# mLSTM head normalization on GpSimd instead of ScalarE, with the heads' transposes one visit later

## The chip, the cores and the metric

The kernel runs on one core of a Trainium2 chip. The metric is the device time of one execution in microseconds; the median of three runs is compared. One execution more was recorded by the hardware profiler, and all durations below come from it. The engines are called as in the profile: PE (TensorE matmul), PEld (its weight loads), DVE (VectorE), ACT (ScalarE), POOL (GpSimd), SP (SyncE, which only issues transfers here).

## What is computed

One inference step of a two-layer streaming encoder over 1024 prompt rows and 32 sample rows, width 1024, all in float32. Layer 0 mixes by an mLSTM with 4 heads (key width 128, value width 256), layer 1 by attention over a band of chunks; each has an MLP with squared ReLU. The change lies in the mLSTM mixer, and within it in the last steps of each head:

```
num = einsum(s, v) + a * einsum(C, q)              # per chunk and head
den = s.sum + a * einsum(n, q)
h   = num / max(|den|, exp(-m_t))
mu  = h.mean(-1);  var = square(h - mu).mean(-1)   # over the 256 values of a head
h   = (h - mu) * rsqrt(var + 1e-6) * mhn_g
h   = h * sigmoid(o_pre)
y   = h @ w_out
```

The division by the denominator and the normalization over 256 values come to one scale and one shift for each row, so that the kernel applies both in one operation `hn * w + b`.

## The kernel before

The input projection of the mLSTM runs head by head. For head h, `qk_proj` makes the queries and keys (six blocks of 24 matmuls, 384, 384 and 288 columns wide, for q and for k), `v_proj` the values (nine tiles of 24 matmuls with 256 columns), and `o_proj` later the output gates, for two heads at a time. While PE does this for head h+1, the mLSTM of head h is done in between: `mlstm(h, ...)` is a Python generator, and after each block or tile of the projection `flow.tick()` advances it by one visit. The rows of a head are nine chunks: eight of 128 prompt rows and one with the 32 sample rows (chunk 8). `flow.finish(ml)` runs what is left of a generator at the end of its head.

A visit i of the loop at the end of `mlstm` does up to four things, each for another chunk:

- `scores(i)`: W = exp(...) on ACT (L666), S = k q and the transpose of k on PE (L668, L669) into one PSUM tile of the tag "tp", their product on DVE (L671), the scaled queries `qc` on POOL (L675), the weighted keys `kw` on ACT (L677).
- `values(i - 1)`: the numerators `num` (L686, L688) and the state's update `cu` (L690) on PE, into PSUM tiles of the tag "nm"; the new state on DVE (L693); mean and variance of the numerators on DVE (L705, L706); a copy of them into the SBUF tile `hn` on ACT (L708), and of the denominator (L709). With every third chunk `values` calls `scales`.
- `state_out(i - 2)`: only for the last two chunks, the transposed state `co` to memory. `co` shares the tag "hn", which has four buffers.
- `heads(c)`: two transposes of `hn` on PE (L738) into a "tp" tile, and a copy into G on ACT (L739). In visits 4, 7 and 10 it is done for two chunks, in 5, 8 and 11 for the third of the group.

`scales` works for three chunks at once on tiles of three columns: five DVE operations (L715 to L719), Ln and Exp on ACT (L720, L721), six DVE operations (L722 to L727). Then it normalizes the three `hn` in place, one operation each (L731). So the transposes of a group of three chunks hang on a chain DVE, ACT, DVE, ACT, and there are 4 heads x 3 groups = 12 such chains and 36 normalizations.

Three rings matter: "tp" has two PSUM buffers, for which S and the heads' transposes take turns; "nm" has two, for `num` and `cu`; "hn" has four SBUF buffers, so that the copy of a fifth chunk's numerators waits for the transposes of the first. For the next head, `mlstm` loads a tile `rc` by DMA and masks it on POOL (two affine_select, L645) before its first visit; W of that head reads it.

The order in which the instructions stand on an engine is not that of the code. The framework's planner lists the instructions by their dependencies, its own planned durations and the order of the code: an instruction that it does not expect to be ready is passed by later ones of the same engine that are. Once listed, an engine takes its instructions strictly in that order. In this stage the order on PE is the planner's.

The numbers of lines are those of the profile.

Of the kernel before, what the change touches and what calls it, by code (L numbers as in the profile page):

```python
# [10 lines left out]
AF = mybir.ActivationFunctionType  # L11
ALU = mybir.AluOpType
# [9 lines left out]
NT = T // P + 1  # L22
# [53 lines left out]
def trunk_kernel(ctx: ExitStack, tc: tile.TileContext, a, o):  # L76
    nc = tc.nc
# [6 lines left out]
    def raw_tile(shape, name):  # L84
        return ring.tile(shape, F32, tag="raw", name=name, bufs=3)
# [93 lines left out]
    def tpt(name):  # L179
        return pa.tile([P, 512], F32, tag="tp", name=name, bufs=2)  # L180
# [458 lines left out]
    def mlstm(h, qT, kT, vts):  # L639
# [10 lines left out]
        def geo(c):  # L650
            return (CH, c * CH, c * CH) if c < NCK else (TS, TP + 3, TP)

        def scores(c):
            L, yo, to = geo(c)
            if c == NCK:
                cl = raw_tile([P, 2, P], f"cl_{h}")
                nc.sync.dma_start(cl, a["state_C"][0, 0, h].rearrange("(j p) k -> p j k", p=P))
                ps = tpt(f"clp_{h}")
                for j in range(2):
                    nc.tensor.transpose(ps[:, j * P:(j + 1) * P], cl[:, j], ident)  # L660
                c0 = A.tile([P, 258], F32, tag="ct", name=f"ct0_{h}", bufs=3)
                nc.vector.tensor_copy(c0[:, :256], ps[:, :256])
                nc.gpsimd.tensor_copy(c0[:, 256:257], n0c[:, h:h + 1])
                live["c0"] = c0
            W = A.tile([P, P], F32, tag="W", name=f"W_{h}_{c}", bufs=3)
            nc.scalar.activation(W[:L, :L], rc[:L, 0, to:to + L], AF.Exp, bias=ae[:L, c, h:h + 1])  # L666
            pst = tpt(f"S_{h}_{c}")
            nc.tensor.matmul(pst[:L, :L], kT[:, yo:yo + L], qT[:, yo:yo + L], start=True, stop=True)  # L668
            nc.tensor.transpose(pst[:L, 256:256 + P], kT[:, yo:yo + L], ident)  # L669
            sT = A.tile([P, P], F32, tag="sT", name=f"sT_{h}_{c}", bufs=2)  # L670
            nc.vector.tensor_mul(sT[:L, :L], pst[:L, :L], W[:L, :L])  # L671
            qc = None
            if c > 0:
                qc = A.tile([P, P], F32, tag="qc", name=f"qc_{h}_{c}", bufs=2)
                nc.gpsimd.tensor_mul(qc[:, :L], qT[:, yo:yo + L], rc[:, 1, to:to + L])  # L675
            kw = A.tile([P, P], F32, tag="kw", name=f"kw_{h}_{c}", bufs=2)
            nc.scalar.activation(kw[:L], pst[:L, 256:256 + P], AF.Copy, scale=W[:L, L - 1:L])  # L677
            live[c] = (sT, qc, kw)

        def values(c):  # L680
            L, yo, to = geo(c)
            sT, qc, kw = live[c]
            vt = vts[c]
            prev = live["c0"] if c == NCK else ct.get(c - 1)
            num = nmt(f"num_{h}_{c}")
            nc.tensor.matmul(num[:L, :257], sT[:L, :L], vt[:L, :257], start=True, stop=qc is None)  # L686
            if qc is not None:
                nc.tensor.matmul(num[:L, :257], qc[:, :L], prev[:, :257], start=False, stop=True)  # L688
            cu = nmt(f"cu_{h}_{c}")
            nc.tensor.matmul(cu[:, :257], kw[:L, :], vt[:L, :257], start=True, stop=True)  # L690
            cn = ct[c] = A.tile([P, 258], F32, tag="ct", name=f"ct_{h}_{c}", bufs=3)
            if prev is not None:
                nc.vector.scalar_tensor_tensor(cn[:, :257], prev[:, :257], albc[:, h, c:c + 1], cu[:, :257],  # L693
                                               op0=ALU.mult, op1=ALU.add)
            else:
                nc.vector.tensor_copy(cn[:, :257], cu[:, :257])

            slot = c % 3
            if slot == 0:
                live["sm"] = A.tile([P, 3, 8], F32, tag="sm", name=f"sm_{h}_{c}", bufs=2)  # L700
                if c + 3 > NCK:
                    nc.gpsimd.memset(live["sm"], 1.0)
            sm = live["sm"]
            st = A.tile([P, 6], F32, tag="st", name=f"st_{h}_{c}", bufs=3)
            nc.vector.bn_stats(st[:L], num[:L, :256])  # L705
            nc.vector.bn_aggr(sm[:L, slot, 0:2], st[:L])  # L706
            hn = live[c] = A.tile([P, 256], F32, tag="hn", name=f"hn_{h}_{c}", bufs=4)
            nc.scalar.copy(hn[:L], num[:L, :256])  # L708
            nc.scalar.copy(sm[:L, slot, 2:3], num[:L, 256:257])  # L709
            if slot == 2:  # L710
                scales(c - 2, sm)

        def scales(c0, sm):
            mean, var, d, rd, v, y0, w, b = (sm[:, :, i] for i in range(8))
            nc.vector.scalar_tensor_tensor(rd, d, -1.0, ae[:, c0:c0 + 3, 32 + h], op0=ALU.mult, op1=ALU.max)  # L715
            nc.vector.tensor_max(rd, rd, d)
            nc.vector.reciprocal(rd, rd)
            nc.vector.tensor_mul(v, var, rd)
            nc.vector.tensor_mul(v, v, rd)  # L719
            nc.scalar.activation(y0, v, AF.Ln, bias=eps_hn)  # L720
            nc.scalar.activation(y0, y0, AF.Exp, scale=-0.5)  # L721
            nc.vector.tensor_mul(w, y0, y0)  # L722
            nc.vector.scalar_tensor_tensor(w, v, HN_EPS, w, op0=ALU.add, op1=ALU.mult)
            nc.vector.tensor_scalar(w, w, -0.5, 1.5, op0=ALU.mult, op1=ALU.add)
            nc.vector.tensor_mul(w, w, y0)
            nc.vector.tensor_mul(w, w, rd)
            nc.vector.scalar_tensor_tensor(b, mean, -1.0, w, op0=ALU.mult, op1=ALU.mult)  # L727
            for i in range(3):
                L = geo(c0 + i)[0]
                hn = live[c0 + i]  # L730
                nc.scalar.activation(hn[:L], hn[:L], AF.Identity, bias=sm[:L, i, 7:8], scale=sm[:L, i, 6:7])  # L731

        def heads(c):
            L, yo, to = geo(c)
            hn = live.pop(c)
            pth = tpt(f"hT_{h}_{c}")
            for j in range(2):
                nc.tensor.transpose(pth[:, j * P:j * P + L], hn[:L, j * P:(j + 1) * P], ident[:L, :L])  # L738
            nc.scalar.copy(G[:, 2 * h:2 * h + 2, to:to + L], pth[:, :256].rearrange("p (j t) -> p j t", j=2)[:, :, :L])  # L739

        def state_out(c):
            if c >= NCK - 1:
                w = 0 if c == NCK - 1 else 1
                nc.gpsimd.tensor_copy(ncol[:, 4 * w + h:4 * w + h + 1], ct[c][:, 256:257])
                ps = tpt(f"co_{h}_{c}")
                for j in range(2):
                    nc.tensor.transpose(ps[:, j * P:(j + 1) * P], ct[c][:, j * P:(j + 1) * P], ident)
                co = A.tile([P, 256], F32, tag="hn", name=f"co_{h}_{c}", bufs=4)
                nc.scalar.copy(co, ps[:, :256])
                nc.sync.dma_start(o["C_s" if w else "C_p"][0, 0, h].rearrange("(j p) k -> p j k", p=P),  # L750
                                  co.rearrange("p (j k) -> p j k", j=2))

        for i in range(NT + 3):
            if i < NT:
                scores(i)
            if 1 <= i <= NT:
                values(i - 1)
            if 2 <= i < NT + 2:
                state_out(i - 2)
            if i >= 4 and i % 3:  # L760
                for c in (i - 4, i - 3)[:3 - i % 3] if i % 3 == 1 else (i - 3,):
                    heads(c)
            yield

    def tick(*_):
# [60 lines left out]
    for h in range(1, NH):  # L826
        unit = [0]

        def after_qk():
            unit[0] += 1  # L830
            if h > 1 or unit[0] >= 3:
                flow.tick()
        if h == 1:
            ml = flow.add(mlstm(0, *qk[0], vts[0]))
        qk.append(qk_proj(h, after_qk))
        vts.append(v_proj(h, tick))
        flow.finish(ml)
        ml = flow.add(mlstm(h, *qk[h], vts[h]))
# [937 lines left out]
    bias, sbias = [], []  # L1776
# [141 lines left out]
    for gp in range(2):  # L1918
        for i in range(17):
            c = slim[gp][i // 2] if i % 2 else wide[i // 2] if i < 16 else slim[gp][8]  # L1920
            if not gp and i < 2:
                c = 7 + i
# [244 lines left out]
```

## Time and profile before

| | us |
|---|---|
| median of three runs | 2409.23 (2408.87 to 2410.61) |
| the profiled execution | 2412.41 |
| its span, first to last instruction | 2410.6 |
| granted TensorE clock, mean | 0.995 of full speed |
| stretch with the visits of `mlstm` | 110 to 386 |

Two kinds of rows are used below. A row of the waits reads "engine, tile and line that waited, what released it: us in total, times, longest". A row of the timeline reads "start, length, engine, line, operation, out <- in, shapes, how many", with the idle time before it and what ended that in brackets. PE's matmuls are pipelined: the length of one is longer than the distance to the next, so that the distance from start to start tells more.

### The profile page before, as it was taken

The numbers are of one execution on the slowest core, as the hardware profiler recorded it, in microseconds if no ns is written. First come the engines' busy times: TensorE is split into PE (matmuls) and PEld (weight loads), VectorE is DVE, ScalarE is ACT, GpSimd is POOL, SyncE is SP. The second block draws the span as 40 slices with busy tenths as digits, with TensorE's granted clock in tenths as the row PEclk, the third lists the DMA queues.
The fourth block names the chain that finished last, engine by engine and source line by source line (L and its number), as shares of the span: only waits on it lengthen the run. The fifth ranks groups of instructions, "written<-read, shape, count | busy, mean of one in ns | idle before, by whom it ended". The sixth has DMA issues, their size and how long they took to land. (4 is left out here: it accounts for less than half of the span.)

```text
span 2410.6 us, 44188 instructions
## 1 busy us (share of the span) xinstructions
PE 2342.7 (97%) x17180; PEld 2250.4 (93%) x17180; DVE 1939.0 (80%) x3903; ACT 1206.0 (50%) x2454; POOL 168.1 (7%) x320
## 2 busy tenths in 40 slices
PE   7999999999999999999999999999999999899997
PEld 4999999999999999999999987789999999899997
DVE  4888766778788789989888777756998889888778
ACT  4565557278666630101147467773776777222212
POOL 0111100000000000000000224420000000000003
PEclk9999999999999999999999999999999999999999
DMA  8343222526566896675512330051486779976642
GB/s 302 120 131 103 78 89 66 177 91 206 184 198 200 279 336 230 252 261 215 183 56 89 82 93 1 10 140 59 165 278 211 259 278 335 355 256 236 224 146 73
DMA packets 284277, 424.64 MB, mean 176 GB/s; under 512 B 15384, under 2 KB 205228, under 8 KB 278948
## 3 DMA queue, kind: packets, MB, share of 16 engines
q1 hardware_dynamic: 279860, 391.48, 48.3%
q10 hardware_dynamic: 4208, 30.35, 3.1%
q8 instruction: 135, 2.21, 0.4%
q14 instruction: 74, 0.61, 0.1%
HBM read 305.96 MB, written 118.17 MB: 176 GB/s over the span
## 5 line engine op out<-in xcount | busy, mean ns | idle before, releaser
L1082 DVE SCALAR_TENSOR_TENSOR ACX<-dn,ada,ACX 128x264 f32<-128x264 f32 (+6 forms) x664 | 281.8, 447 | 83.2 <-PE dn L1452 41.1
L1452 PE MATMUL dn<-fx,wf_d 128*128 128x264 f32 x2016 | 254.1, 285 | 6.8 <-DVE ACX L1082 3.5
L1452 PEld LDWEIGHTS dn<-fx,wf_d 128*128 128x128 f32 x2016 | 248.8, 188 | 9.0 <-DVE ACX L1082 3.0
L89 ACT CAST w_dn<-raw_dn 128x1024 fp32r<-128x1024 f32 x36 | 37.7, 1050 | 282.1 <-DVE aw L279 136.9
L118 PE MATMUL dn<-hs,w_dn 128*128 128x384 f32 (+2 forms) x512 | 161.2, 315 | 0.0
L119 PE MATMUL dn<-hs,w_dn 128*128 128x384 f32 (+2 forms) x512 | 161.0, 315 | 0.0
L120 PE MATMUL dn<-hs,w_dn 128*128 128x384 f32 (+2 forms) x512 | 156.4, 314 | 1.3 <-DVE w_dn L90 1.3
L1317 PE MATMUL up<-TF,wf_u 128*128 128x264 f32 x1056 | 143.2, 285 | 3.8 <-ACT H L1320 3.8
L1317 PE MATMUL up<-U,wf_u 128*128 128x264 f32 x1056 | 140.3, 285 | 1.7 <-ACT H L1320 1.2
L1317 PE MATMUL up<-u,wf_u 128*128 128x264 f32 x1056 | 139.7, 285 | 1.3 <-ACT wf_u L89 0.7
L279 DVE SCALAR_TENSOR_TENSOR aw<-radw,cs,aw 128x512 f32<-128x512 f32 x196 | 139.5, 743 | 1.1 <-DMA radw<-in_w_ada_dram 1.1
L1317 PEld LDWEIGHTS up<-TF,wf_u 128*128 128x128 f32 x1056 | 134.4, 189 | 4.8 <-ACT H L1320 4.6
L1317 PEld LDWEIGHTS up<-U,wf_u 128*128 128x128 f32 x1056 | 133.0, 188 | 3.0 <-ACT H L1320 1.6
L1317 PEld LDWEIGHTS up<-u,wf_u 128*128 128x128 f32 x1056 | 132.9, 188 | 1.9 <-ACT wf_u L89 0.9
L118 PE MATMUL dn<-U,w_dn 128*128 128x384 f32 (+2 forms) x416 | 129.4, 312 | 0.6 <-DVE ada L304 0.6
L119 PE MATMUL dn<-U,w_dn 128*128 128x384 f32 (+2 forms) x416 | 129.4, 312 | 0.0
L120 PE MATMUL dn<-U,w_dn 128*128 128x384 f32 (+2 forms) x416 | 125.9, 313 | 0.6 <-DVE w_dn L90 0.5
L1817 ACT ACTIVATE p<-p,mx 128x576 f32<-128x576 f32 (+9 forms) x132 | 86.6, 657 | 27.5 <-DVE mx L1814 25.2
L120 PEld LDWEIGHTS dn<-hs,w_dn 128*128 128x128 f32 x512 | 96.0, 188 | 2.0 <-DVE w_dn L90 1.8
L118 PEld LDWEIGHTS dn<-hs,w_dn 128*128 128x128 f32 x512 | 96.5, 189 | 0.1
L119 PEld LDWEIGHTS dn<-hs,w_dn 128*128 128x128 f32 x512 | 96.6, 189 | 0.0
L90 DVE TENSOR_TENSOR HL<-H,HL 128x1056 fp32r<-128x1056 f32 x64 | 80.3, 1254 | 20.0 <-ACT HL L89 19.9
(403 smaller groups left out, 7111.0 us busy)
## 6 DMA issues: line engine op xcount, KB each, us to landing
hpl<-HL SPq DMA_DIRECT2D x144, 264.0 KB
rdn_u<-in_w_up_dram SPq DMA_DIRECT2D x64, 512.0 KB
hd<-HL SPq DMA_DIRECT2D x28, 1056.0 KB
fx<-hd SPq DMA_DIRECT2D x50, 528.0 KB
radw<-in_w_ada_dram SPq DMA_DIRECT2D x24, 1024.0 KB
hd<-HM SPq DMA_DIRECT2D x28, 792.0 KB
raw_up<-in_w_up_dram SPq DMA_DIRECT2D x40, 512.0 KB
raw_dn<-in_w_down_dram SPq DMA_DIRECT2D x36, 512.0 KB
```

The lines of the kernel that those rows point to most:

```text
L89: nc.scalar.copy(dst_h, src)
L90: (eng or nc.vector).tensor_sub(dst_l, src, dst_h.bitcast(F32))
L118: nc.tensor.matmul(ps, wh, mov(0, k), start=(k == 0), stop=False)
L119: nc.tensor.matmul(ps, wh, mov(1, k), start=False, stop=False)
L120: nc.tensor.matmul(ps, wl, mov(0, k), start=False, stop=(k == nk - 1))
L279: nc.vector.scalar_tensor_tensor(acc[cnd], raw[:, k], sc, acc[cnd], op0=ALU.mult, op1=ALU.add)
L1082: nc.vector.scalar_tensor_tensor(xs, ps[:, off + o:off + o + mm_], gate[:, fc, cnd:cnd + 1], xs, op0=ALU.mult, op1=ALU.add)
L1317: nc.tensor.matmul(p, self.ws[w][:, wl, k], moving(f, tp, xl, k), start=first and k + n_ == 0, stop=k == 3 and n_ == 2, skip_group_check=n ...
L1452: nc.tensor.matmul(p, ws[w][:, wl, k], t[:, s0, xl], start=first and k + n_ == 0, stop=k == kg - 1 and n_ == 2, skip_group_check=not first)
L1817: nc.scalar.activation(z, z, AF.Exp, bias=mx[:, 0:1], scale=-1.0, accum_out=mx[:, 1:2])
```

## The change

The normalization in `scales` moves from ACT to POOL (`tensor_scalar` with two operands that hold one value for each row). `heads` moves by one visit, from 4, 5, 7, 8, 10 and 11 to 5, 6, 8, 9, 11 and 12, and within the visit from the end to the place between `scores` and `values`. The loop has one visit more.

```diff
@@ -728,7 +728,7 @@
             for i in range(3):
                 L = geo(c0 + i)[0]
                 hn = live[c0 + i]
-                nc.scalar.activation(hn[:L], hn[:L], AF.Identity, bias=sm[:L, i, 7:8], scale=sm[:L, i, 6:7])
+                nc.gpsimd.tensor_scalar(hn[:L], hn[:L], sm[:L, i, 6:7], sm[:L, i, 7:8], op0=ALU.mult, op1=ALU.add)
@@ -750,16 +750,16 @@
-        for i in range(NT + 3):
+        for i in range(NT + 4):
             if i < NT:
                 scores(i)
+            if i >= 5 and i % 3 != 1:
+                for c in (i - 5, i - 4) if i % 3 == 2 else (i - 4,):
+                    heads(c)
             if 1 <= i <= NT:
                 values(i - 1)
             if 2 <= i < NT + 2:
                 state_out(i - 2)
-            if i >= 4 and i % 3:
-                for c in (i - 4, i - 3)[:3 - i % 3] if i % 3 == 1 else (i - 3,):
-                    heads(c)
             yield
```

The 36 operations, their operands and the transposes themselves stay as they were.

## The prediction

> **What bounds the kernel now.** I read the busy shares first, then the table by stretch, then the waits.
>
> ```profile
> PE 2342.7 (97%) x17180; PEld 2250.4 (93%) x17180; DVE 1939.0 (80%) x3903; ACT 1206.0 (50%) x2454; POOL 168.1 (7%) x320
> 110.00:150.00 40.00, 39.74 (x272) 37.84 (x271) 39.59 (x89) 29.16 (x84) 5.42 (x22) 1.00 0.25 75
> 150.00:250.00 100.00, 97.36 (x671) 90.51 (x671) 82.15 (x193) 53.15 (x150) 14.55 (x41) 1.00 0.41 127
> 250.00:386.00 136.00, 134.59 (x874) 126.21 (x873) 95.77 (x246) 80.42 (x220) 13.74 (x38) 1.00 0.28 87
> 386.00:2410.00 2024.00, 1978.37 (x14791) 1920.19 (x14789) 1652.51 (x3236) 987.43 (x1891) 121.75 (x187) 1.00 0.54 184
> ```
>
> The columns of the stretches are length, then busy time of PE, PEld, DVE, ACT and POOL, granted clock, DMA share, GB/s. The mLSTM visits lie between 110 and 386 us. There PE is busy 39.74 + 97.36 + 134.59 = 271.69 of 276 us, at a granted clock of 1.00; DVE is full only in the first 40 us, ACT has 113 us free and POOL 242. After 386 us PE is busy 1978 of 2024 us. So TensorE sets the end throughout, and the change can gain only what PE waits for in the mLSTM stage. What that is:
>
> ```profile
> PEld hT L738 <- ACT hn L731: 6.5, 11, 1.5
> PE hT L738 <- ACT hn L731: 3.5, 4, 1.3
> PEld co L747 <- issue: 1.3, 4, 0.3
> PEld S L668 <- DVE y L617: 0.5, 1, 0.5
> ```
>
> The first two rows are the waits of weight load and matmul for the same event (total us, times, longest): the transposes of L738 wait for the ACT normalization of L731, in 11 of the 12 groups of three chunks, 6.5 us at most by the weight load. No other wait of PE or PEld in this stretch comes to more than 1.3 us, and the one longest wait for DVE is 0.5. **6.5 us, 0.27% of the span, is the ceiling.** L731 in its turn needs L727, the last of the small DVE operations in `scales`.
>
> How do these waits arise? Three views of one place, head 0, chunks 3 to 5 (start, length, instruction):
>
> ```profile
> 153.85 1.06 DVE L727 SCALAR_TENSOR_TENSOR sm<-sm 128x3 f32<-128x3 f32 x1
> 154.83 0.74 DVE L279 SCALAR_TENSOR_TENSOR ada_acc<-ada_room,cs,ada_acc 128x512 f32<-128x512 f32 x1
> ```
> ```profile
> 153.73 3.89 POOL L645 TENSOR_SCALAR_AFFINE_SELECT rc<-rc 128x1024 f32<-128x1024 f32 x2 [4.17 <-DMA rc<-rc_d]
> ```
> ```profile
> 154.92 0.40 ACT L666 ACTIVATE W<-rc,ae 128x128 f32<-128x128 f32 x1 [3.72 <-POOL rc L645]
> 155.23 1.57 ACT L731 ACTIVATE hn<-hn,sm 128x256 f32<-128x256 f32 x3
> ```
> ```profile
> 154.29 0.28 PE L489 MATMUL v<-w_v,U 128*128 128x256 f32 x1
> 154.40 0.28 PE L487 MATMUL v<-w_v,U 128*128 128x256 f32 x1
> 155.87 0.44 PE L738 MATMUL hT<-ident,hn 128*128 128x128 f32 x2 [1.19 <-ACT hn L731]
> ```
>
> PE runs projection matmuls 0.11 us apart until 154.40 and then has the transpose at its head, which can start at 155.87: 1.47 - 0.12 = 1.35 us are lost. L727 ended at 154.91, ACT then still had a W of the next head, the first normalization ran from 155.23 to 155.82, and PE went on 0.05 us later. So the transposes stand in PE's queue where the planner expected the normalization, and PE pays for each lateness.
>
> **Does the transpose move at all?** This decides more than the engine. In head 1 the code emits `heads(0)` in visit 4, ahead of the fifth numerators, which belong to visit 5. The trace has:
>
> ```profile
> 199.59 0.70 PE L686 MATMUL num<-vt,sT 128*128 128x257 f32 x2
> ...
> 200.56 0.60 PE L690 MATMUL cu<-vt,kw 128*128 128x257 f32 x2
> ...
> 205.10 0.28 PE L489 MATMUL v<-w_v,U 128*128 128x256 f32 x1
> 205.44 0.44 PE L738 MATMUL hT<-ident,hn 128*128 128x128 f32 x2
> ```
> ```profile
> L487 PE MATMUL v<-w_v,U 128*128 128x256 f32 x12 | 3.6, 296 | 0.0
> L489 PE MATMUL v<-w_v,U 128*128 128x256 f32 x12 | 3.4, 280 | 0.0
> L488 PE MATMUL v<-w_v,U 128*128 128x256 f32 x12 | 3.4, 280 | 0.0
> ```
>
> The fifth numerators stand ahead of the first transposes, and 36 projection matmuls (12 of each line between 200.7 and 205.3 us) lie between them; one v tile has 24. The planner has already put these transposes past the place to which the change moves them, because their input is not expected earlier. A later place in the code then binds nothing: PE has always some other matmul, and the transpose comes when the planner expects its input. Counting the numerators in the trace in this way, the new place lies behind the old one in two of the twelve groups only: the last of head 2 and the second of head 3.
>
> ```profile
> 295.56 0.28 PE L489 MATMUL v<-w_v,U 128*128 128x256 f32 x1
> 296.20 0.44 PE L738 MATMUL hT<-ident,hn 128*128 128x128 f32 x2 [0.36 <-ACT hn L731]
> ```
> ```profile
> 357.43 0.29 PE L119 MATMUL o<-U,w_o 128*128 128x288 f32 x1
> 357.87 0.44 PE L738 MATMUL hT<-ident,hn 128*128 128x128 f32 x2
> ```
>
> **The change part by part.** The rows for prices (ns: min/median/max, or mean):
>
> ```profile
> L731 ACT ACTIVATE hn<-hn,sm x36: 584/588/604, 142.6 to 377.7; 128x256 f32<-128x256 f32 x32, 32x256 f32<-32x256 f32 x4
> L1825 POOL TENSOR_SCALAR p<-p,mx 128x320 f32<-128x320 f32 x8 | 4.2, 532 | 4.3 <-DVE mx L1823 4.3
> L1825 POOL TENSOR_SCALAR p<-p,mx 128x192 f32<-128x192 f32 x8 | 3.3, 426 | 1.1 <-DVE mx L1823 1.1
> L675 POOL TENSOR_TENSOR qc<-y,rc x32: 240/458/1479, 105.0 to 354.3; 128x128 f32<-128x128 f32 x28, 128x32 f32<-128x32 f32 x4
> L675 POOL TENSOR_TENSOR qc<-y,rc 128x128 f32<-128x128 f32 x26 | 15.0, 577 | 79.4 <-PE num L688 78.8 <-DMA rc<-rc_d 0.6
> L719 DVE TENSOR_TENSOR sm<-sm x12: 121/157/420, 135.5 to 371.2; 128x3 f32<-128x3 f32 x12
> L727 DVE SCALAR_TENSOR_TENSOR sm<-sm x12: 123/166/1060, 142.4 to 376.5; 128x3 f32<-128x3 f32 x12
> ```
>
> *Place.* The two moved groups lose their waits: 0.64 - 0.12 = 0.52 and 0.44 - 0.12 = 0.32, together **-0.8 us**. What moves with a head is two transposes and one ACT copy into G, no DMA.
>
> *Engine.* 36 x 588 ns = 21 us leave ACT, which is half idle here, so that this is worth nothing in itself. On POOL one normalization should take halfway between the 426 and 532 ns of the neighbouring widths, 0.48 us (its second operation is a real addition here, which the row does not show; ends 0.43 and 0.59). Each remaining waiting group (11 - 2 = 9) gets its first chunk 0.588 - 0.48 = 0.11 us sooner: **-1.0 us**.
>
> *Queue on POOL.* The normalization waits for L727 at the head of POOL. Behind it stand `qc` (its 79 us of waiting for PE show that it is made about a visit ahead of its numerators), the two-column memsets of `vt`, the copies of `tails`, and the next head's affine_select of L645, for which that head's W on ACT waits, and the rest of ACT behind that. All but the last have a visit of slack. The other way round costs more: in the place shown above ACT runs the next head's W, which needs L645, ahead of the normalization, so the planner expects L645 first, and the normalization queues behind it. L645 ended at 157.62; plus 0.48 that is 158.10 instead of 155.82, or +2.3 us of PE wait. The order on POOL in the changed kernel is not shown, the ends are 0 and 2.3; I take half, **+1.2 us**. At the other two boundaries:
>
> ```profile
> 218.65 2.45 POOL L645 TENSOR_SCALAR_AFFINE_SELECT rc<-rc 128x1024 f32<-128x1024 f32 x2 [3.73 <-DMA rc<-rc_d]
> ...
> 287.66 1.25 POOL L645 TENSOR_SCALAR_AFFINE_SELECT rc<-rc 128x1024 f32<-128x1024 f32 x2 [3.47 <-ACT hn L731]
> ```
> ```profile
> 220.96 0.62 DVE L727 SCALAR_TENSOR_TENSOR sm<-sm 128x3 f32<-128x3 f32 x1
> ```
> ```profile
> 287.03 1.10 ACT L731 ACTIVATE hn<-hn,sm 128x256 f32<-128x256 f32 x2 [1.50 <-DVE sm L727]
> ```
>
> In head 1 L645 ended (221.10) before L727 did (221.58), in head 2 it began after the normalization: nothing there.
>
> *Port.* `qc` takes 458 ns by the median and 577 by the mean of this stretch: 0.12 us of delay beside DVE. For the nine groups of heads 0 to 2, less the one priced above, 8 x 0.12 = **+1.0 us**; ends 0 and the rival below. DVE is delayed too: L719 took 420 instead of 157 ns at worst, and 36 x 0.26 = 9.5 us of DVE time is the bound; PE hardly waits for DVE in this stretch, so I put 0 on the path, and up to 3 us in heads 0 and 1 if the DVE slack is gone.
>
> *Buffers.* `hn` has four buffers; with heads 6 to 8 held longer, the state copy `co` of visit 10 has only the buffer of the other `co` and waits for its DMA on ACT. A v tile of 24 x 0.12 = 2.8 us on PE covers that, 0 us; uncovered it is 1 us per head, by the longest of the two such waits that the kernel has now:
>
> ```profile
> ACT co L749 <- DMA out_dram<-co: 1.4, 2, 1.0
> ```
>
> *Planner.* How long it expects the POOL operation to take is not in the trace. If longer than the chip takes, every transpose comes later in PE's queue and its wait shrinks; if shorter, it grows. I take 0; ends -5 and +2 us. The stages after 386 us are replanned as well; their 46 us of PE idle may shift by a few per cent, 2 us either way.
>
> Sum: -0.8 - 1.0 + 1.2 + 1.0 = +0.4 us. The profiled execution took 2412.41 us for its span of 2410.6, so it would take 2412.8; the median of the runs is 3.18 us lower, 2409.23, and becomes **2409.6 us**. 0.2% (4.8 us) is about what a measurement of this kernel can tell from no change, so the forecast is: no change.
>
> **The rivals.**
>
> *All waits go.* If the planner allows POOL more time than it takes, or the order of the moved transposes falls better than my count, the waits vanish: about -6 us (6.5 less the 0.05 us of signal in each of 11), 2403.2 us. For it: without the 1.35 us above, the mean of the others is 0.5 us, so little is needed. Against it: the largest come from late DVE and POOL work, which stays.
>
> *GpSimd late by its queue (slower).* If at each of the three head boundaries the affine_select lands ahead of the normalization as priced for head 0, that is 3 x 2.3 + 1.0 - 1.8 = +6.1 us, 2415.3. It decides from the point at which the normalization starts over 1 us after L727 has ended. Against it: two of the three boundaries show no collision now.
>
> *GpSimd late by the port (slower).* In the place above L727 begins while L645 runs and takes 1.06 us instead of 0.17; L645 in turn took 3.89 us beside DVE. If each first normalization of heads 0 to 2 waits for one two-input DVE operation such as L279 (0.74 us), that is 9 x 0.74 = 6.7, with -1.8 and +1.2 in all +6.1 us, 2415.3 again. The Trainium skill, SBUF — State Buffer, section "Who interferes with whom", states this as a lock: GpSimd shares a port pair with VectorE, and a VectorE instruction with two SBUF inputs and a GpSimd instruction that reads SBUF exclude each other for a whole instruction, whichever starts first. The two rows agree with it; by that rule alone the change would come out slower. The median of `qc`, 458 ns in a stage in which DVE is 79% busy, says that most instructions escape, so it is a rival only.
>
> **How the numbers follow.** Forecast, within 0.2%: 0.60, its own range 2405 to 2414. All waits go: 0.22. Queue: 0.09, port: 0.09. The range takes in the centre of the first rival and most of the way to the other two: 2403 to 2414.5. Faster by over 0.2%: 0.22; within: 0.60; slower: 0.18.
>
> **What would show it.** The first transpose of head 1 still after the fifth numerators, near 205 us: the place does not bind. The wait of hT then names POOL instead of ACT, with 4 to 8 us in total. A normalization on POOL of 0.43 to 0.6 us, longer where DVE is full. Head 0's second group late behind L645, by up to 3.7 us on PE. I am wrong if the wait of hT is gone (below 1 us), if PE newly waits for ACT or DVE in this stage, or if stages after 386 us change by more than 3 us.

## The result, and the profile after

The changed kernel takes 2423.89 us (median of 6 runs, 2418.34 to 2426.57) beside 2409.05 us before (2408.44 to 2414.3): a ratio of 1.0058, interval 1.0048 to 1.0068. It is 14.8 us slower, above the predicted range (2403 to 2414.5). The profiled execution has a span of 2424.8 us.

Where the time went is read from windows that end just behind the last transposes of the mLSTM, at 379 us before and at 394 us after. The columns are those of the prediction: length, busy time of PE, PEld, DVE, ACT and POOL, granted clock, DMA share, GB/s. First the kernel before:

```profile
110.00:379.00 269.00, 264.69 (x1772) 247.70 (x1770) 214.59 (x518) 158.90 (x443) 33.71 (x101) 1.00 0.32 100
```

The changed kernel, this stretch and 2024 us behind it:

```profile
110.00:394.00 284.00, 270.45 (x1771) 251.97 (x1770) 215.05 (x518) 144.19 (x410) 60.46 (x137) 0.98 0.31 97
400.00:2424.00 2024.00, 1978.65 (x14797) 1922.37 (x14795) 1650.98 (x3237) 987.19 (x1891) 122.38 (x187) 1.00 0.54 184
```

The stretch is 15.0 us longer, and the 2024 us behind it hold what 2024 us held before (PE 1978.65 us busy, before 1978.37). All of the loss lies in the mLSTM stage. It has two parts: PE is idle 284.00 - 270.45 = 13.55 us instead of 4.31 (+9.2), and it is busy 5.8 us longer with the same number of matmuls (1771 and 1772), at a mean clock of 0.98 instead of 1.00. ACT got 14.7 us lighter, which is worth nothing here.

The waits of the changed kernel in this stage name the event that the prediction watched, now released by POOL (us, times, longest; before 6.5 and 3.5):

```profile
PEld hT L738 <- POOL hn L731: 17.7, 17, 3.2
```
```profile
PE hT L738 <- POOL hn L731: 12.5, 10, 2.7
```

One GpSimd normalization, by its line and then by stretch, heads 0 to 2 first and head 3 below:

```profile
L731 POOL TENSOR_SCALAR hn<-hn,sm x36: 544/555/1577, 141.9 to 392.2; 128x256 f32<-128x256 f32 x32, 32x256 f32<-32x256 f32 x4
```
```profile
L731 POOL TENSOR_SCALAR hn<-hn,sm 128x256 f32<-128x256 f32 x24 | 20.0, 841 | 22.2 <-DVE sm L727 22.2
```
```profile
L731 POOL TENSOR_SCALAR hn<-hn,sm 128x256 f32<-128x256 f32 x9 | 5.0, 568 | 18.1 <-DVE sm L727 18.1
```

Undisturbed it takes 0.555 us, about ACT's 0.588. In head 3 the mean is near that (0.568; one of the nine belongs to the end of head 2), in heads 0 to 2, where VectorE prepares the next head's weights and the ada products, it is 0.841.

The costliest place shows how this becomes time. The third group of head 0 in the changed kernel, as three timelines (PE, POOL, DVE):

```profile
166.95 0.28 PE L489 MATMUL v<-w_v,U 128*128 128x256 f32 x1
169.97 1.22 PE L738 MATMUL hT<-ident,hn 128*128 128x128 f32 x4 [2.75 <-POOL hn L731]
```
```profile
168.53 2.45 POOL L731 TENSOR_SCALAR hn<-hn,sm 128x256 f32<-128x256 f32 x3 [4.72 <-DVE sm L727]
```
```profile
166.45 1.22 DVE L90 TENSOR_TENSOR w_v<-raw_v,w_v 128x1024 fp32r<-128x1024 f32 x1
167.59 0.16 DVE L724 TENSOR_SCALAR sm<-sm 128x3 f32<-128x3 f32 x1
...
168.18 0.17 DVE L727 SCALAR_TENSOR_TENSOR sm<-sm 128x3 f32<-128x3 f32 x1
168.26 1.22 DVE L90 TENSOR_TENSOR w_v<-raw_v,w_v 128x1024 fp32r<-128x1024 f32 x1
```

PE had the transpose at its head from 167.2 us, when VectorE was still in L90 with four of the small operations of `scales` to come. L727 ended at 168.35. POOL started 0.18 us later, in the shadow of the next L90 (168.26 to 169.48). Its three operations took 2.45 us. The first was done just ahead of the transpose at 169.97, some 1.4 us after its start (2.45 less twice 0.55) and 0.4 us after that L90 had ended. At 0.56 us it would have been done some 0.8 us earlier.

What follows on PE, in windows of 3.41 us of the same kernel:

```profile
166.75:170.16 3.41, 0.66 (x7) 0.47 (x5) 2.64 (x6) 1.05 (x1) 1.63 (x2) 1.00 0.74 225
170.16:173.57 3.41, 3.41 (x16) 2.79 (x16) 2.02 (x4) 1.16 (x4) 0.82 (x2) 0.50 0.88 278
173.57:176.98 3.41, 3.41 (x20) 3.41 (x21) 2.17 (x4) 1.19 (x2) 0.00 (x0) 1.00 0.01 2
```

After 2.75 us of idling PE works for 3.41 us at half the clock. The stage of the changed kernel has three such spells, from 170.16, 211.12 and 231.59 us, the first and the last after the two longest gaps; the stage before has none. They hold 3.41 + 3.41 + 6.83 = 13.65 us, so they cost at most 6.8 us, and the 5.8 us of longer busy time fit that. The Trainium skill, TensorE: Matmul & The Clock Gate, Part 1, states a gate of half or full rate, set by the activity in windows of about 3.4 us; the length and the 0.50 agree with it.

### The profile page after: what moved, and what is told of

Its sections match the earlier page's. It is cut to its first block, busy times and chain, and to the rows that moved or that the text cites. A ratio compares the mean times of both kernels' runs of the same rounds, so it can differ in the third digit from the quotient of the medians.

```text
span 2424.8 us, 44232 instructions
## 1 busy us (share of the span) xinstructions
PE 2346.8 (97%) x17180; PEld 2255.8 (93%) x17180; DVE 1937.3 (80%) x3903; ACT 1189.9 (49%) x2418; POOL 192.0 (8%) x356
## 3 DMA queue, kind: packets, MB, share of 16 engines
q8 instruction: 135, 2.21, 0.4%
## 5 line engine op out<-in xcount | busy, mean ns | idle before, releaser
L90 DVE TENSOR_TENSOR HL<-H,HL 128x1056 fp32r<-128x1056 f32 x64 | 80.2, 1254 | 20.4 <-ACT HL L89 20.4
```

Source lines behind the costliest of these rows:

```text
L90: (eng or nc.vector).tensor_sub(dst_l, src, dst_h.bitcast(F32))
```

## The experiments

Theories. **A**: GpSimd's normalization comes late against the place at which the planner put the transposes: the planner expects it earlier, VectorE's two-input operations stretch it, and the gaps on PE bring half-clock spells. **B**: the moved transposes cost. **C**: GpSimd's mere presence beside VectorE costs. Ratios are to runs of the kernel before on the same chip (medians 2408.26 for e1 to e4, 2409.07 for e5, e6, e9 and e10, 2408.70 for the rest).

### Each half of the change alone: e1_engine, e2_place

e1 is the kernel before with the operation moved to POOL, e2 the changed kernel with it put back on ACT.

```diff
-                nc.scalar.activation(hn[:L], hn[:L], AF.Identity, bias=sm[:L, i, 7:8], scale=sm[:L, i, 6:7])
+                nc.gpsimd.tensor_scalar(hn[:L], hn[:L], sm[:L, i, 6:7], sm[:L, i, 7:8], op0=ALU.mult, op1=ALU.add)
```

> The kernel before with the normalization on GpSimd; the transposes stay where they were. Theory A (the added time comes from the GpSimd normalization: it ends later than the planner placed the transposes for, PE stands at hT, and the granted clock halves after such gaps): 2417 to 2426 us, wait of hT for POOL 12 us or more. Rival B (the moved transposes do it, by the order of S, num and cu and the two PSUM buffers): 2409 us within 3, wait of hT about 6.5 us as before.

> The changed kernel with the normalization back on ScalarE; the transposes stay one visit later, ahead of the numerators. A: 2406 to 2412 us, wait of hT for ACT 4 to 8 us, no half-clock spell between 110 and 386 us. B: 2417 us or more with the wait of hT well above 6.5 us.

Measured: e1 2428.18 us, ratio 1.0083 (1.0068 to 1.0098); e2 2404.71, 0.9992 (0.9983 to 1.0002). The waits and the stage of e1, then of e2:

```profile
PEld hT L738 <- POOL hn L731: 20.3, 25, 2.1
```
```profile
110.00:394.00 284.00, 269.19 (x1760) 249.95 (x1759) 213.71 (x516) 143.99 (x408) 59.94 (x137) 0.98 0.31 97
```
```profile
PEld hT L738 <- ACT hn L731: 4.9, 7, 1.2
```
```profile
110.00:377.00 267.00, 263.71 (x1771) 247.24 (x1770) 213.88 (x518) 158.15 (x445) 34.79 (x101) 1.00 0.33 103
```

The engine alone costs 19.9 us (PE idle 14.81 us, and three half-clock spells of 3.41 us), the place alone gives 3.6 back (its interval just takes in no change, and its stage has no such spell); the sum, 16.4, is near the 14.8 of the change. B falls.

Why the wait grows without a collision can be counted in e1, where the transposes have their old place in the code. Between the fifth numerators and the first transposes of head 1 stand

```profile
L487 PE MATMUL v<-w_v,U 128*128 128x256 f32 x11 | 3.3, 297 | 0.0
L489 PE MATMUL v<-w_v,U 128*128 128x256 f32 x11 | 3.1, 280 | 0.0
L488 PE MATMUL v<-w_v,U 128*128 128x256 f32 x11 | 3.1, 279 | 0.0
```

33 projection matmuls, where the kernel before had 36. The planner lists these transposes 3 x 0.117 = 0.35 us earlier, as if the normalization were faster on POOL, and on the chip it is not. The same count from fixed numerators over all twelve groups has them two or three PE instructions earlier in seven groups and 12 earlier in one, at the same place in one and 2 to 10 later in three: a tendency, not a rule.

### Another engine, a later place: e3_dve, e4_two, e6_act_two, e12_dve_place, e13_place_again

e3 is the kernel before with the operation on VectorE (first diff). e4 and e6 move the transposes two visits instead of one, with POOL and with ACT; e12 is the changed kernel with VectorE, e13 is e2 again.

```diff
-                nc.scalar.activation(hn[:L], hn[:L], AF.Identity, bias=sm[:L, i, 7:8], scale=sm[:L, i, 6:7])
+                nc.vector.tensor_scalar(hn[:L], hn[:L], sm[:L, i, 6:7], sm[:L, i, 7:8], op0=ALU.mult, op1=ALU.add)
```
```diff
-        for i in range(NT + 3):
+        for i in range(NT + 5):
...
+            if i >= 6 and i % 3 != 2:
+                for c in (i - 6, i - 5) if i % 3 == 0 else (i - 5,):
+                    heads(c)
```

> The kernel before with the normalization on VectorE, transposes as before. If it is an engine beside DVE's chain (a signal to another engine, the shared port) that is late, DVE itself, which ended the chain anyway, has neither: wait of hT 6.5 us or less, 2404 to 2410 us. If any move away from ScalarE is late because the planner counts the operation too short, the wait rises as in e1: 2415 us or more.

> The changed kernel (GpSimd) with the transposes one visit later still (visits 6, 7, 9, 10, 12, 13). If one visit did not bind because the planner expects the input later than that place, and two visits do bind: wait of hT below 5 us and 2406 to 2412 us. If the planner's expectation still decides, or the four hn buffers now hold up the numerators: wait of hT 10 us or more, 2416 us or more.

> Normalization on ScalarE as before, the transposes two visits later than before and ahead of that visit's numerators (one visit later still than in the changed kernel). Theory A: with ScalarE the place binds in five of the twelve groups and their waits are gone; hT waits 3 to 4.5 us, no half-clock spell in the stage, 2402 to 2406 us. Rival: the longer hold of the four hn buffers delays the copies and with them the numerators: 2408 or more, with PE waiting for num or co.

> Normalization on VectorE with the transposes at the changed kernel's place. Theory A: VectorE needs 0.40 us for one and follows its own last small operation without a signal between engines, so hT waits 3 to 5 us, no half-clock spell; 2402 to 2406 us, like e2_place or a little better. Rival: VectorE, over 80 per cent busy in heads 0 and 1, is delayed by 36 x 0.4 us more: 2407 or more, with PE waiting for VectorE.

> e2_place once more, in five rounds beside e12_dve_place: 2403 to 2406 us, hT waits 4 to 6 us for ScalarE. If the gain of the place alone is real, its interval lies below 1.0000; if it was chance, it holds 1.0000.

e3: 2410.70 us, 1.0008 (0.9999 to 1.0018). On VectorE the operation is the shortest of the three, hT waits less than before, so that not every move away from ScalarE is late; but the time doesn't follow, and stays just above the expected 2404 to 2410:

```profile
PEld hT L738 <- DVE hn L731: 5.0, 6, 1.5
```
```profile
L731 DVE TENSOR_SCALAR hn<-hn,sm x36: 376/406/752, 141.2 to 377.0; 128x256 f32<-128x256 f32 x32, 32x256 f32<-32x256 f32 x4
```

e4: 2416.50, 1.0033 (1.0023 to 1.0042), 12.5 us of hT by the weight load, as the second of the two expectations had it. In head 0 the second group is one of five that now stand behind the place at which their input is ready, and PE goes on without a gap:

```profile
155.97 0.29 PE L489 MATMUL v<-w_v,U 128*128 128x256 f32 x1
156.09 0.60 PE L738 MATMUL hT<-ident,hn 128*128 128x128 f32 x4
```

Where the place binds, PE waits for GpSimd in none of the five; in the other groups the planner still puts the transposes where it expects their input, and they wait.

e6: 2409.82, 0.9999 (0.9989 to 1.0009): a miss. hT waits little (4.6 us), but one gap of 3.40 - 2.21 = 1.19 us, no larger than one that had no consequence in the kernel before (last section), brought 6.8 us at half clock:

```profile
286.20:289.60 3.40, 2.21 (x14) 1.19 (x14) 1.05 (x7) 2.73 (x10) 0.40 (x3) 1.00 0.00 0
289.60:296.40 6.80, 6.80 (x27) 5.34 (x27) 2.71 (x14) 2.87 (x11) 0.76 (x6) 0.50 0.00 0
```

e12: 2413.13, 1.0014 (1.0003 to 1.0025), a miss too. The plan differs again, and PE meets waits of a size that no other kernel had:

```profile
PE hT L738 <- ACT G L739: 3.8, 1, 3.8
PE hT L738 <- DVE hn L731: 2.8, 3, 1.6
PE num L686 <- DVE ct L693: 1.4, 1, 1.4
```

The idling ahead of 225.74 us, 2.70 us in 3.42, was followed by 6.8 us at half clock, which cost up to 3.4 us of the 4.4 that e12 is above the kernel before.

e13: 2406.29, 0.9987 (0.9978 to 0.9996), though hT waits 6.1 us in its profile: one gap in head 0 was 2.18 us long, in the profile of e2 0.97, and here 3.41 us at half clock followed. ScalarE with the new place is the best version found, by 2.4 to 3.6 us; the first series could not tell it from no change, the second just does. How much of it is the shorter wait stays open.

### GpSimd's load off the path: e5_beside, e11_spare

Both add 36 operations of the same size on POOL to the kernel before. e5 writes them into G ahead of the heads' copy; e11 does them in place on `hn` once the transposes have read it.

```diff
                 nc.scalar.activation(hn[:L], hn[:L], AF.Identity, bias=sm[:L, i, 7:8], scale=sm[:L, i, 6:7])
+                to = geo(c0 + i)[2]
+                nc.gpsimd.tensor_scalar(G[:L, 2 * h:2 * h + 2, to:to + L], hn[:L, :2 * L].rearrange("p (j t) -> p j t", j=2),
+                                        sm[:L, i, 6:7], sm[:L, i, 7:8], op0=ALU.mult, op1=ALU.add)
```
```diff
             nc.scalar.copy(G[:, 2 * h:2 * h + 2, to:to + L], pth[:, :256].rearrange("p (j t) -> p j t", j=2)[:, :, :L])
+            ws = live.pop(('s', c))
+            nc.gpsimd.tensor_scalar(hn[:L], hn[:L], ws[:L, 6:7], ws[:L, 7:8], op0=ALU.mult, op1=ALU.add)
```

> The kernel before, with 36 more GpSimd operations of the same size at the same places: they read hn beside ScalarE's normalization, which stays as it is, and write into G, where the heads' copy overwrites them later (extra work, nothing left out). Theory A (what costs is the lateness of the operation on the path to the transposes): nobody waits for the added operations but the copies into G; within 3 us of before, hT waits 6 to 9 us for ACT. Rival C (GpSimd's presence costs, by delaying VectorE's two-input operations through the shared port): 8 us or more over before, with hT waiting over 12 us for ACT or PE waiting for DVE.

> The kernel before with 36 more GpSimd operations of the same form and size, in place on hn after the chunk's transposes have read it; nothing but the reuse of the buffer a visit later waits for them (extra work, nothing left out). Theory A (the lateness on the path to the transposes costs, not GpSimd's load): hT waits 5 to 8 us for ScalarE, PE idle in the stage 3.5 to 6 us, 2407 to 2412 us. Rival C (GpSimd beside VectorE delays VectorE and through it PE): 2415 us or more with PE waiting for VectorE's results.

e5: 2418.36 us, 1.0044 (1.0027 to 1.0061), as C has it. But PE waits for ScalarE's normalization as long as before (3.5 us), never for VectorE, and newly for the copies into G:

```profile
PE hT L741 <- ACT hn L731: 3.5, 4, 1.3
PE clp L660 <- ACT G L742: 2.3, 2, 1.8
PE S L668 <- ACT G L742: 1.5, 2, 1.3
```
```profile
157.00:160.50 3.50, 1.64 (x14) 1.16 (x13) 1.40 (x5) 1.53 (x7) 2.95 (x6) 1.00 0.01 2
160.50:170.70 10.20, 10.20 (x40) 7.37 (x39) 6.41 (x19) 3.92 (x12) 1.34 (x5) 0.50 0.28 81
```

The copy into G had to wait for the added operation (1.81 us at 158.87 us), so it held the PSUM buffer that `S` and `clp` needed, and the gap brought 10.2 us at half clock. So e5 does not isolate the load: its operations were on the path after all. e11 takes them off it: 2410.38, 1.0010 (1.0001 to 1.0019).

```profile
PEld hT L739 <- ACT hn L732: 6.4, 11, 1.4
```
```profile
L742 POOL TENSOR_SCALAR hn<-hn,sm x36: 544/556/2019, 143.9 to 380.5; 128x256 f32<-128x256 f32 x32, 32x256 f32<-32x256 f32 x4
```

The same operations, one of them stretched to 2.02 us and their mean in heads 0 to 2 at 0.757 (e1: 0.850), cost 1.7 us in all (by the interval 0.2 to 4.6) where nobody waits for them, and no half-clock spell stands in the stage. C falls but for those 1.7 us: not the load costs, but the lateness on the path.

### The planner's part and the port's: e8_head3, e9_one_pool, e10_one_act

e8 uses POOL in head 3 alone, at the old place. e9 is e1, and e10 the kernel before, both with three two-input operations of VectorE put as one-input ones, which leaves out the sums that they made (one of the three in the second diff):

```diff
+                if h == 3:
+                    nc.gpsimd.tensor_scalar(hn[:L], hn[:L], sm[:L, i, 6:7], sm[:L, i, 7:8], op0=ALU.mult, op1=ALU.add)
+                else:
+                    nc.scalar.activation(hn[:L], hn[:L], AF.Identity, bias=sm[:L, i, 7:8], scale=sm[:L, i, 6:7])
```
```diff
-                        nc.vector.scalar_tensor_tensor(acc[cnd], raw[:, k], sc, acc[cnd], op0=ALU.mult, op1=ALU.add)
+                        nc.vector.tensor_scalar(acc[cnd], raw[:, k], sc, None, op0=ALU.mult)
```

> GpSimd normalizes in head 3 alone, at the old place; heads 0 to 2 stay on ScalarE. In head 3 no projection runs beside it and VectorE has few operations with two SBUF inputs, so only the planner's part is left there. Theory A: the first operations of the three groups take 0.55 to 0.7 us, the transposes still wait 0.3 to 0.5 us longer for each group and 0.2 to 0.3 us for the second chunk; hT waits 2 to 3 us more than the 6.5 of before, the time is 1 to 3 us over before. Rival (the port is all): head 3 as before, hT 6.5 us, no difference in time.

> GpSimd normalization at the old place, as in e1_engine, but three of VectorE's operations with two SBUF inputs (L90, L279, L611) are put as operations with one SBUF input (leaves out: the low parts of the split weights, the sums of the ada product and of the convolution). To be compared with e10_one_act, the same with ScalarE's normalization. Theory A (planner part about 7 us, port about 5.6, half clock the rest): no first normalization of a group over 0.8 us unless another two-input operation stands beside it; e9 8 to 14 us over e10. Rival (the port does it all): e9 within 4 us of e10. Rival (the port does nothing to the end): e9 18 us or more over e10.

> Control for e9_one_pool: the kernel before with the same three VectorE operations put as operations with one SBUF input (leaves out the same sums). hT waits 4 to 7 us for ACT; the time is 2395 to 2412 us.

e8: 2412.01 us, 1.0017 (1.0008 to 1.0026). Head 3 in the kernel before, then in e8, with e8's operations below:

```profile
PEld hT L738 <- ACT hn L731: 1.8, 3, 1.1
```
```profile
PEld hT L741 <- POOL hn L732: 4.3, 7, 1.7
```
```profile
L732 POOL TENSOR_SCALAR hn<-hn,sm x9: 544/554/679, 340.6 to 380.0; 128x256 f32<-128x256 f32 x8, 32x256 f32<-32x256 f32 x1
```

With hardly a stretched operation, three groups wait 2.5 us more. That is the part of the place and the signal alone: PE has 29, 59 and 85 instructions ahead of the three transposes, counted from fixed numerators, where the kernel before had 31, 61 and 85, and in heads 0 to 2 the counts are those of before. The time says less, because in this execution head 0, where ScalarE still normalizes, had a gap of 1.86 us instead of 1.19 and a half-clock spell of 3.41 us.

e9: 2399.23, 0.9965 (0.9955 to 0.9976); e10: 2393.29, 0.9937 (0.9922 to 0.9952). e9, its normalization in heads 0 to 2 and its stage, then e10:

```profile
PEld hT L737 <- POOL hn L730: 13.8, 23, 1.8
```
```profile
L730 POOL TENSOR_SCALAR hn<-hn,sm 128x256 f32<-128x256 f32 x24 | 14.2, 605 | 29.1 <-DVE sm L726 29.1
```
```profile
110.00:380.00 270.00, 260.73 (x1737) 242.21 (x1736) 169.04 (x504) 139.69 (x399) 48.42 (x137) 0.99 0.31 96
```
```profile
PEld hT L737 <- ACT hn L730: 7.3, 10, 2.2
```
```profile
110.00:374.00 264.00, 258.59 (x1727) 242.12 (x1726) 165.85 (x499) 151.26 (x426) 24.92 (x101) 0.99 0.30 95
```

The same group in e1:

```profile
L731 POOL TENSOR_SCALAR hn<-hn,sm 128x256 f32<-128x256 f32 x24 | 20.2, 850 | 27.2 <-DVE sm L727 19.1 <-ACT vt L494 7.8
```

Without most of the two-input operations GpSimd's mean falls from e1's 0.850 to 0.605 us, and moving the operation costs 5.9 us (2399.23 - 2393.29) instead of 19.9. PE's idle time grows by 9.27 - 5.41 = 3.9 us instead of 14.81 - 4.31 = 10.5. The two ratios leave the 5.9 us open by some 4 either way, and VectorE is 45 to 49 us lighter in both kernels. Half-clock spells differ as well: in the profiled executions e10 has two of 3.41 us in the stage, after gaps of 2.02 and 1.84 us before ScalarE's results, and e9 one, which flatters GpSimd by up to 1.7 us. So the shares are rough. Still, the planner's part with the signal is about 6 us of 20, and about 14 go with the two-input operations: the stretched normalizations, and the half clock that follows longer gaps. A had put the port's part too low (its 8 to 14 us between e9 and e10 was a miss).

## Why the prediction was wrong, step by step

**What bounds the kernel** was right: PE sets the end, and hT is the only wait of its matmuls that came to more than 0.5 us. But the 6.5 us were a ceiling for the gain only; nothing in the trace bounded the loss. (The 11 waits fall in 10 of the 12 groups, one of which waits twice; that changes the engine term by 0.1 us.) Of the signs that were named, the place and the length of the normalization came as said; the wait of hT, 17.7 us where 4 to 8 were expected, did not.

***Place*, -0.8 us.** The reading that the planner, not the code, sets the place was right. In the changed kernel the first transposes of head 1 still come behind the fifth numerators:

```profile
203.89 0.60 PE L686 MATMUL num<-vt,sT 128*128 128x257 f32 x2
...
209.41 0.44 PE L738 MATMUL hT<-ident,hn 128*128 128x128 f32 x2 [0.53 <-ACT vt L494]
```

Alone it measured -3.6 and -2.4 us (e2, e13), the first within the noise: the right sign, and more than the term.

***Engine*, -1.0 us.** The operation takes 0.555 us, not 0.48, within the ends; from L727's end to the first result it takes 0.66 to 0.74 us where nothing disturbs it, and ACT took 0.64. The term is zero at best.

***Queue*, +1.2 us.** At the named place it did not happen: in head 0 the normalization ran at 152.18 us, ahead of L645. It happened in head 1 instead:

```profile
225.48 3.09 POOL L645 TENSOR_SCALAR_AFFINE_SELECT rc<-rc 128x1024 f32<-128x1024 f32 x2 [1.32 <-DMA rc<-rc_d]
228.55 0.44 POOL L675 TENSOR_TENSOR qc<-y,rc 128x128 f32<-128x128 f32 x1
228.94 0.09 POOL L495 MEMSET vt<- 128x2 f32 x1
229.02 2.04 POOL L731 TENSOR_SCALAR hn<-hn,sm 128x256 f32<-128x256 f32 x3
```
```profile
226.10 1.08 DVE L727 SCALAR_TENSOR_TENSOR sm<-sm 128x3 f32<-128x3 f32 x1
```

L727 ended at 227.18 us, POOL got to the normalization 1.84 us later, and PE idled 2.73 us. At the third boundary L645 did not come between. That the term's +1.2 us is near what it cost is chance: the place that was priced is not the one that paid.

***Port*, +1.0 us** is the first of three steps that failed. The price of 0.12 us a group was the difference between mean and median of `qc`, an operation that may start at any time. The normalization may not: it starts the moment L727 lets go, which is the moment VectorE, 78% busy in heads 0 to 2 with long two-input operations behind its small ones, starts the next of them. In the changed kernel five of the nine first operations in heads 0 to 2 took 0.97 us or more. The slower rival named this mechanism. It was given 0.09 because of a median that did not apply, and its price lacked the clock. With the half clock that follows, about 14 of e1's 20 us go with the two-input operations. The Trainium skill, SBUF — State Buffer, section "Who interferes with whom", states the lock by which the change would come out slower; the L90 rows agree with it, the first result coming some 0.4 us after L90's end.

***Planner*, 0 us (ends -5 and +2)** is the second. At the same place in the code the planner lists the transposes of most groups earlier when POOL normalizes (33 matmuls instead of 36 in the one shown), and the wait grows even where nothing collides: +2.5 us in head 3 alone (e8), which is over the end of +2, and about 6 us in all (e9 against e10, open by some 4). That the planned length was unknown was said; that with a wait in 10 of the 12 groups already no slack was left to take up an error was not.

***Buffers*, 0 us**, and the stages after 386 us (2 us either way): right, neither shows a change.

**A term was missing**, which is the third. The sum took PE's gaps as they are, with no price for the clock. In the changed kernel they brought 13.65 us at half clock, 5.8 us more of busy time, which alone is more than a third of the loss.

## What to carry to other kernels

An operation that others wait for is not priced by its duration on an idle engine. On GpSimd, look at what VectorE does at the moment its input becomes ready: if that is a long operation with two SBUF inputs, expect the result only some time after that operation has ended, as behind L90 here. Where a planner places the consumer, moving the producer to another engine changes the plan as well, so count the matmuls ahead of the consumer in both traces before you explain a wait. On a PE-bound stage add up to half of each half-clock spell to gaps of over a microsecond; here 1.6 us of idling within one window of 3.41 us nearly always brought a spell.

## What the runs showed of the hardware

Short gaps were enough for the half clock. Idle times of 1.2 to 2.75 us in 3.4 us were followed by spells of 3.41, 6.8 and 10.2 us. Not each was: in the kernel before, 3.41 - 2.22 = 1.19 us of idling had no consequence, the same amount as in e6.

```profile
153.80:157.21 3.41, 2.22 (x19) 1.95 (x18) 3.41 (x6) 2.29 (x6) 3.41 (x2) 1.00 0.63 222
157.21:160.60 3.39, 3.39 (x21) 1.98 (x20) 3.01 (x7) 2.87 (x10) 1.98 (x5) 1.00 0.52 147
```

The Trainium skill, TensorE: Matmul & The Clock Gate, Part 1, names a whole idle window of about 3.4 us as the condition, and a window that runs free. The first is not what these runs show. The second agrees with the traces: the three spells of the changed kernel begin 40.96 and 20.47 us apart, which is 12 and 6 times 3.413 us, and in each of the 14 traces all changes of the clock lie on one grid of 3.413 us.

On these grids, from 105 to 400 us, PE was idle for 1.6 us or more in 14 windows at full clock, and 13 of them were followed by half clock. Of 14 windows with 1.1 to 1.5 us of idling two were followed by it, and none with less. The 1.19 us of the kernel before and of e6 both lie within one window of their grid, so that the phase of the window does not explain why this pair ended differently; that stays open.

Two executions of one kernel can differ by such a spell, as the profiles of e2 and e13 do. The changed kernel spread over 8 us in six runs, at mean clocks of 0.991 to 0.995.
